# A decoder trunk on one core: four pairs of weight buffers and three fetch buffers instead of three and four, two slots less, and one small fetch moved

## The chip, the cores and the metric

The kernel runs on one NeuronCore of a Trainium2 chip. The core has a matrix engine (TensorE, PE in the profile, with PEld for its weight loads), a vector engine (VectorE, DVE), an engine for activation functions (ScalarE, ACT), a general one (GpSimd, POOL) and a queue engine (SyncE, SP) that only issues DMA transfers. The metric is the device time of one execution in microseconds (us); lower is better. A kernel is timed in several runs, and the median is given.

## The reference

One layer of a hybrid decoder over 512 tokens of width 1024, in float32. `mixed` stands for the three token mixers that share one input projection:

```python
h = rms_norm(x, norm_mix)
z_rnn, z_q, z_k, z_v, z_g, z_dec, z_mq, z_gate = split(h @ w_in)
# 1: recurrence: conv of width 4, gates of 8 blocks, scan over the tokens
xr = causal_dwconv(z_rnn, rnn_conv_w, rnn_conv_b)
out_a = rg_lru(xr, rg_w_a, rg_b_a, rg_w_x, rg_b_x, rg_lambda)
# 2: gated linear attention, 4 heads of 96, values of 192
log_alpha = log_sigmoid(z_dec @ gla_w_decay + gla_b_decay) / 16
o = chunked_gla(z_q, z_k, z_v, log_alpha)
out_b = rms_norm(o, gla_norm) * silu(z_g)
# 3: attention of 4 heads of 192 to a memory of 256 rows
out_c = softmax_attention(z_mq, rms_norm(mem, mem_norm) @ w_mem_kv)
proj = [out_n @ w_branch[n] for n in range(3)]
x = x + sum(sigmoid(z_gate[n]) * proj[n]) @ w_out
# gated MLP of width 3072 with a causal conv of width 3
up = causal_dwconv(rms_norm(x, norm_ffn) @ w_up, ffn_conv_w, ffn_conv_b)
x = x + (gelu(gate_half(up)) * value_half(up)) @ w_down
return rms_norm(x, final_norm)
```

`z_dec` has 16 columns per token, and `gla_w_decay` is a matrix of 16 x 384: the decay logits' weights.

## The kernel before, in words

**Heads and rests.** Each float32 operand is split into a head, rounded to the format that PE multiplies fast (`hi`, `whi`), and the rest (`lo`, `wlo`). A product is made of three matmuls: head by head, head by rest, rest by head (`mm3`, L104). `split` makes the head with a copy on ACT (L97) and the rest with a subtraction on DVE (L98).

**Units and steps.** The program is first laid out as a list `prog` of units and steps. A unit is one block of weights with its matmuls, for instance 128 output channels of a projection: 24 matmuls of 512 columns. `fetch` (L166) takes a fetch buffer (`raw`, 4 KB a partition, `NRAW` = 4 of them), issues the load on SP's queue, takes a pair `whi`, `wlo` (`NWB` = 3 pairs) and splits into it. `emit` places this fetch and split `AHEAD` = 2 units before the unit that uses them, and the steps (evacuations, scans, norms) stand between the units. From this order the framework's scheduler makes the order on each engine at compile time; it may put a later instruction first where an earlier one isn't ready by its own reckoning. On the chip each engine works through its own fixed order. A buffer is taken again when the last reader of what lay in it is done.

**Slots.** All other large intermediates share one pool of `NSLOT` = 53 slots of 2 KB a partition (`fslot` for float32, `rslot` for heads and rests).

**Products with seven multiplications.** The values (`wv`), the gate of the linear attention (`wg`) and most of the down projection are computed by blocks with seven products instead of eight (`seven`, L285 on). Weights are needed singly (`direct`, L303, into a fetch buffer) and as sums of quarters: `load` (L294) fetches a quarter into two slots on SP's queue, and `add` (L299) adds further quarters in flight, as an accumulating DMA on POOL's queue. For `wv` and `wg` the direct quarters are fetched 4 units ahead (`far`). The heads' sums on the other side are made and split on DVE and ACT (L774 to L791, `h_ready`).

**Order of the stages.** Memory keys and values; input projections with the attention to the memory woven between; the recurrence, woven with the gates and projections of the third branch (`b2`); then the stage of the linear attention, in which `wv` and `wg` are woven with gates and projections of the first branch (`g0`, `p0`); then the rest of the branches, the output projection, the up and the down projections.

**The decay weights.** At the start of the linear attention's stage stands the step `decay_weights` (L865 to L873). It takes a slot of 80 rows, clears it on POOL (L867), loads the 16 x 384 matrix three times into it from SP's queue (L869), makes the head on ACT (L871) and the rest of the last 16 rows on DVE (L873). The first matmul with it is `decay_logit` (L894), some 100 us later. The recurrence's stage ends with `lru_decay(1)` (exponentials on ACT), `lru_square`, `lru_root` and `lru_scan` for the blocks 4 to 7; the scan's results are copied on POOL's queue into other rows (L730).

Of the kernel before, what the change touches and what calls it, by code (L numbers as in the profile page):

```python
# [27 lines left out]
H = 4  # L28
DK = 96
DV = 192  # L30
CH = 64
LOW = 16
KZ = 5 * LOW
# [1 line left out]
NF = FF // P  # L35
EPS = 1e-6
LRU_C = 8.0
NSLOT = 53
NWB = 3
AHEAD = 2  # L40
BRANCHES = (2, 0, 1)
NRAW = 4
HT = S // 2
NWARM = 9

# [12 lines left out]
def trunk(ctx: ExitStack, tc: tile.TileContext, x, xT, mem, memT, par, wdecay, wch, wv, wg, wmk,  # L58
          wmv, wrg, wbr, wout, wup, wdown, wdown2, gffn, gfin, out):
    nc = tc.nc  # L60
    pool = lambda name, bufs, **kw: ctx.enter_context(tc.tile_pool(name=name, bufs=bufs, **kw))
    const = pool("const", 1)
    wpool = pool("wpool", NWB)
    hpool = pool("hpool", 1)
    apool = pool("apool", NSLOT)
    small = pool("small", 4)
# [5 lines left out]
    def nm(s):  # L72
        uid[0] += 1
        return f"{s}_{uid[0]}"

    def fslot(shape=(P, S)):
        return apool.tile(list(shape), F32, tag="s", name=nm("f"))

    def rslot(shape=(P, S)):
        return apool.tile(list(shape), F32R, tag="s", name=nm("r"))  # L80
# [14 lines left out]
    def split(hi, lo, src, eng=None):  # L95

        nc.scalar.activation(hi, src, AF.Copy)  # L97
        (eng or nc.vector).tensor_tensor(out=lo, in0=src, in1=hi.bitcast(F32), op=ALU.subtract)  # L98
# [34 lines left out]
    def unit(dram, n, fn, parts=1):  # L133

        w = {}
        i = sum(1 for k, *_ in prog if k == "unit")

        def ready():
            w["w"] = fetch(dram, n, parts)
            for h in behind.get(i, ()):  # L140
                h()
        prog.append(("unit", [(AHEAD, ready)], lambda: fn(w["w"])))
# [5 lines left out]
    def step(fn):  # L148
        prog.append(("step", [], fn))

    def weave(units, steps, lead=0):

        done, m = 0, max(1, len(units) - lead)
        for i, u in enumerate(units):
            unit(*u)
            upto = len(steps) * max(0, i + 1 - lead) // m
            for s in steps[done:upto]:
                step(s)
            done = max(done, upto)
        for s in steps[done:]:  # L160
            step(s)

    def fetch(dram, n, parts):
        p = dram.shape[0]
        raw = wpool.tile([p, n], F32, tag="raw", name=nm("raw"), bufs=NRAW)
        loads.append(nc.sync.dma_start(raw, dram))  # L166
# [118 lines left out]
    def seven(src, n, np, lhs, pre, read, far=AHEAD):  # L285
# [15 lines left out]
        def direct(q, p):  # L301
            raw[q, p] = wpool.tile([P, 2, n], F32, tag="raw", name=nm("raw"), bufs=NRAW)
            loads.append(nc.sync.dma_start(raw[q, p], src(q, p)))  # L303
# [93 lines left out]
    def start():  # L397

        raw = [wpool.tile([P, D], F32, tag="raw", name=nm("raw"), bufs=NRAW) for _ in range(2)]
        whi, wlo = ([wpool.tile([P, D], F32R, tag=t, name=nm(t)) for _ in range(2)] for t in ("whi", "wlo"))  # L400
# [38 lines left out]
    def mem_load(i):  # L439

        raw = wpool.tile([P, 4, MEM], F32, tag="raw", name=nm("raw"), bufs=NRAW)
        nc.sync.dma_start(raw, memT[:, 4 * i:4 * i + 4, :])
# [247 lines left out]
    def lru_decay(g):  # L690
        bs = range(4 * g, 4 * g + 4)
        for b in bs:
            lru["aw", b] = fslot((DK, S)), fslot((DK, S))
            nc.scalar.activation(lru["aw", b][0], lru[0, b], AF.Exp, scale=lsc[:DK, b:b + 1])
        for b in bs:
            r = lru[0, b]
            lru["last"] = nc.scalar.activation(r, r, AF.Tanh, scale=nsc[:DK, b:b + 1])
# [7 lines left out]
    def lru_root(g):  # L705
        with tc.issue_after(lru["last"].ins):
            for i in range(4):
                w = lru["aw", 4 * g + i][1]
                nc.scalar.activation(w, w, AF.Sqrt)
# [22 lines left out]
    def lru_out(t):  # L732
        oa.append((rslot(), rslot()))
        split(*oa[t], of[t])

    each = lambda fn, bs: [lambda b=b: fn(b) for b in bs]
    lo, hi = range(4), range(4, 8)
    b2 = [u for d in range(KD) for u in branch(2, oc, d)]
# [5 lines left out]
    weave([lru_weights(1)] + b2[4:8], each(lru_square, lo) + [lambda: lru_root(0)] + each(lru_split, hi))  # L744
    weave(b2[8:12], [s for p in zip(each(lru_scan, lo), each(lru_gates, hi)) for s in p])
    step(lambda: lru_decay(1))
    weave(b2[12:], each(lru_square, hi) + [lambda: lru_root(1)] + each(lru_scan, hi))


    HP = 2 * DV  # L750
    flat2 = lambda a: a.rearrange("p a b -> p (a b)")
    gla = {}
    vt = [[None, None] for _ in range(NT)]
    sg = [[None, None] for _ in range(NT)]
    chm = const.tile([DK, S], F32, name="chm")
# [105 lines left out]
    def g_fast():  # L861
        return seven(lambda q, p: wg[p, int(q[1]) - 1, int(q[2]) - 1], HP, 2, h_lhs, {}, g_read, 4)


    def decay_weights():  # L865
        wy = fslot((KZ, H, DK))
        nc.gpsimd.memset(wy, 0.0)  # L867
        for c in range(0, KZ, 2 * LOW):
            nc.sync.dma_start(wy[c:c + LOW], wdecay)  # L869
        r = gla["wy"] = rslot((KZ, H, DK))  # L870
        nc.scalar.activation(r, wy, AF.Copy)  # L871
        lo = slice(4 * LOW, KZ)
        nc.vector.tensor_tensor(out=r[lo], in0=wy[lo], in1=r[lo].bitcast(F32), op=ALU.subtract)  # L873
# [144 lines left out]

    step(causal)
    step(decay_weights)  # L1020
    gates = {}

# [340 lines left out]
```

## Time and profile before

| | |
|---|---|
| median of 3 runs | 940.94 us (940.58 to 941.29) |
| the profiled execution | 941.12 us, of it span 939.4 us |
| granted clock of PE, mean | 0.996 |
| PE busy | 921.3 us, 98% |
| DVE, ACT, POOL busy | 636.6, 488.2, 90.9 us |
| DMA | 116.93 MB, 124 GB/s over the span |

The span runs from the first to the last instruction. A row of a timeline has the start and the duration in us, the engine, the line, the operation, what it writes and reads, and in brackets the idle time of the engine before it with what ended it. PE is busy in 98% of the span, so the time is to be looked for in the few stretches where it isn't, and in the granted clock there.

### The profile page before, as it was taken

Reading aid. Unit: us, or ns where it says so; the run is one execution under the profiler, and the core shown is the slowest. Engines: PE = TensorE matmul, PEld = TensorE weight load, DVE = VectorE, ACT = ScalarE, POOL = GpSimd, SP = SyncE. Lnnn points to the kernel's source line nnn. Section 1 sums busy time; section 2 is a strip of 40 time slices with the busy share of each in tenths; the row PEclk is TensorE's granted clock in tenths of the full one; section 3 lists DMA queues with packets and bytes.
Section 4 is the critical chain, followed back from the end, with each engine's and each line's share of the span. In section 5 each row is a group of like instructions: output and inputs, shape, how many; then the busy total and the mean of one; then the engine's idle time right before and its main releaser. Section 6 shows DMA issues by size and latency. Waiting matters only on the chain.

```text
span 939.4 us, 11996 instructions
## 1 busy us (share of the span) xinstructions
PE 921.3 (98%) x4390; PEld 779.7 (83%) x4390; DVE 636.6 (68%) x1117; ACT 488.2 (52%) x796; POOL 90.9 (10%) x133
## 2 busy tenths in 40 slices
PE   9999999999998999999999999999999999999996
PEld 7899888888877998878888898888888888888885
DVE  6996745565788454795767665555686666698765
ACT  6765555685845345864434424344345444545544
POOL 0000000000053141000000000000010130012102
PEclk9999999999999999999999999999999999999999
DMA  7435223213369594231146401233364685357612
GB/s 250 160 119 196 88 80 108 85 59 106 111 161 186 130 202 135 76 119 51 51 135 225 167 23 45 92 111 112 135 114 138 146 227 119 110 126 184 162 45 89
DMA packets 45562, 116.93 MB, mean 124 GB/s; under 512 B 5520, under 2 KB 12864, under 8 KB 45504
## 3 DMA queue, kind: packets, MB, share of 16 engines
q1 hardware_dynamic: 33152, 94.28, 30.3%
q0 software_dynamic: 11776, 20.85, 13.0%
q10 hardware_dynamic: 576, 1.05, 0.3%
q8 instruction: 34, 0.56, 0.2%
q14 instruction: 24, 0.20, 0.1%
HBM read 111.69 MB, written 3.67 MB: 123 GB/s over the span
## 4 chain that ended last, share of the span: by engine, by line
PE 88%; DVE 6%; ACT 3%; issue 1%; DMA 1%; POOL 0%; SPq 0%; DVEq 0%; ACTq 0%
PE mm L104 81%; PE sm L104 2%; PE mm L419 1%; DVE wlo L98 1%; PE sm L983 1%; DMA m<-in_xT 1%; DVE f L920 0%; PE sm L969 0%; PE sm L604 0%; PE sm L985 0%; PE sm L585 0%; DVE f L774 0%; DMA f<-in_wdecay 0%; DVE r L98 0%; PE sm L956 0%
## 5 line engine op out<-in xcount | busy, mean ns | idle before, releaser
L98 DVE TENSOR_TENSOR wlo<-raw,whi 128x1024 fp32r<-128x1024 f32 (+2 forms) x155 | 172.4, 1115 | 161.0 <-PE mm L104 75.7
L97 ACT ACTIVATE whi<-raw 128x1024 fp32r<-128x1024 f32 (+2 forms) x155 | 149.7, 970 | 173.2 <-PE mm L104 159.5
L104 PE MATMUL mm<-whi,r 128*128 128x512 f32 (+2 forms) x568 | 172.7, 374 | 3.5 <-ACT r L97 1.8
L104 PE MATMUL mm<-h2l,whi 128*128 128x512 f32 x360 | 140.1, 389 | 0.0
L104 PE MATMUL mm<-h2h,whi 128*128 128x512 f32 x360 | 139.9, 389 | 0.0
L104 PEld LDWEIGHTS mm<-whi,r 128*128 128x128 f32 x568 | 106.4, 189 | 19.3 <-DVE r L98 2.3
L104 PE MATMUL mm<-hh,whi 128*128 128x512 f32 x288 | 113.8, 395 | 2.3 <-ACT whi L97 2.3
L104 PE MATMUL mm<-hl,whi 128*128 128x512 f32 x288 | 113.0, 392 | 0.0
L104 PE MATMUL mm<-wlo,r 128*128 128x512 f32 (+2 forms) x284 | 106.2, 374 | 0.4 <-DVE wlo L98 0.4
L104 PE MATMUL mm<-r,whi 128*128 128x512 f32 (+1 forms) x448 | 98.9, 369 | 0.0
L104 PEld LDWEIGHTS mm<-r,whi 128*128 128x128 f32 x448 | 77.8, 189 | 14.1 <-DVE r L98 0.2
L104 PE MATMUL mm<-h2h,wlo 128*128 128x512 f32 x360 | 88.9, 389 | 0.0
L97 ACT ACTIVATE whi<-f 128x512 fp32r<-128x512 f32 (+2 forms) x90 | 48.3, 581 | 74.6 <-PE mm L104 64.5
L104 PEld LDWEIGHTS mm<-h2h,wlo 128*128 128x128 f32 x360 | 67.6, 188 | 14.0
L104 PEld LDWEIGHTS mm<-h2l,whi 128*128 128x128 f32 x360 | 67.6, 188 | 14.0
L104 PEld LDWEIGHTS mm<-h2h,whi 128*128 128x128 f32 x360 | 67.5, 188 | 14.0
L98 DVE TENSOR_TENSOR wlo<-f,whi 128x512 fp32r<-128x512 f32 (+2 forms) x90 | 53.7, 631 | 35.8 <-ACT whi L97 19.6
L299 POOL DMA_DIRECT2D f<-in_wdown x40 | 35.1, 986 | 438.9 <-DVE wlo L98 415.8
L1127 DVE SCALAR_TENSOR_TENSOR f<-mm,prm,f 128x511 f32<-128x511 f32 x96 | 71.4, 745 | 6.9 <-ACT f L1125 6.1
L104 PE MATMUL mm<-hh,wlo 128*128 128x512 f32 x288 | 71.2, 389 | 0.0
L104 PEld LDWEIGHTS mm<-hh,whi 128*128 128x128 f32 x288 | 54.1, 188 | 13.9 <-ACT whi L97 3.0
L104 PEld LDWEIGHTS mm<-hh,wlo 128*128 128x128 f32 x288 | 54.1, 188 | 11.3
(243 smaller groups left out, 1313.2 us busy)
## 6 DMA issues: line engine op xcount, KB each, us to landing
raw<-in_wup SPq DMA_DIRECT2D x48, 512.0 KB, 3.6
raw<-in_wch SPq DMA_DIRECT2D x40, 512.0 KB, 3.6
f<-in_wdown POOLq DMA_DIRECT2D x40, 256.0 KB, 5.3
raw<-in_wbr SPq DMA_DIRECT2D x24, 384.0 KB, 3.1
raw<-in_wdown SPq DMA_DIRECT2D x14, 512.0 KB, 3.7
f<-in_wdown SPq DMA_DIRECT2D x20, 256.0 KB, 4.3
raw<-in_wout SPq DMA_DIRECT2D x8, 512.0 KB, 3.4
f<-in_wv POOLq DMA_DIRECT2D x16, 200.0 KB, 5.6
```

Source lines behind the costliest of these rows:

```text
L97: nc.scalar.activation(hi, src, AF.Copy)
L98: (eng or nc.vector).tensor_tensor(out=lo, in0=src, in1=hi.bitcast(F32), op=ALU.subtract)
L104: nc.tensor.matmul(ps, lhsT=l, rhs=r, start=first and i == 0, stop=last and i == len(seq) - 1, skip_group_check=more)
L299: nc.gpsimd.dma_start(raw[to, p][j], src(q, p)[:, j, :], accum_op=ALU.add)
L419: nc.tensor.matmul(ps[u], lhsT=a, rhs=b, start=q == 0 and i in (0, 2), stop=q == KD - 2 and i >= len(seq) - 2)
L983: nc.tensor.matmul(ps[:, j, :], lhsT=sT[h][:, t, :], rhs=vt[t][hp][:, j, :], start=True, stop=t == 0)
L1127: nc.vector.scalar_tensor_tensor(out=a[:, j:], in0=ps[:, :S - j], scalar=col(C_FCW + 48 * (2 - j) + f), in1=a[:, j:], op0=ALU.mult, op1=AL ...
```

## The change

Four edits. `NWB` goes from 3 to 4: a fourth pair of buffers for heads and rests of weights, 8 KB more a partition. `NRAW` goes from 4 to 3 (4 KB less) and `NSLOT` from 53 to 51 (4 KB less), so that the memory used is the same. The clearing and the three loads of the decay weights go into a new step `decay_load`, which stands in the recurrence's stage after `lru_decay(1)`; the loads are issued on POOL's queue instead of SP's. `decay_weights` keeps its place and its two instructions on ACT and DVE.

```diff
-NSLOT = 53
-NWB = 3
+NSLOT = 51
+NWB = 4
 AHEAD = 2
 BRANCHES = (2, 0, 1)
-NRAW = 4
+NRAW = 3
...
+    gla = {}
+
+
+    def decay_load():
+        wy = gla["raw"] = fslot((KZ, H, DK))
+        nc.gpsimd.memset(wy, 0.0)
+        for c in range(0, KZ, 2 * LOW):
+            nc.gpsimd.dma_start(wy[c:c + LOW], wdecay)
+
...
     step(lambda: lru_decay(1))
+    step(decay_load)
     weave(b2[12:], each(lru_square, hi) + [lambda: lru_root(1)] + each(lru_scan, hi))
...
     def decay_weights():
-        wy = fslot((KZ, H, DK))
-        nc.gpsimd.memset(wy, 0.0)
-        for c in range(0, KZ, 2 * LOW):
-            nc.sync.dma_start(wy[c:c + LOW], wdecay)
+        wy = gla.pop("raw")
         r = gla["wy"] = rslot((KZ, H, DK))
         nc.scalar.activation(r, wy, AF.Copy)
```

More of the change, by code (lines that the diff above doesn't have):

```diff
@@ L751, in trunk @@
     flat2 = lambda a: a.rearrange("p a b -> p (a b)")
-    gla = {}
     vt = [[None, None] for _ in range(NT)]
```

## The prediction

> **What bounds the kernel now.** I read the totals first, then the busy time of the engines by stretches of 20 us, then each engine's timeline where the first engine shows idle time.
>
> ```profile
> span 939.4 us, 11996 instructions
> PE 921.3 (98%) x4390; PEld 779.7 (83%) x4390; DVE 636.6 (68%) x1117; ACT 488.2 (52%) x796; POOL 90.9 (10%) x133
> ...
> 260.00:280.00 20.00, 18.61 (x91) 16.34 (x89) 17.21 (x27) 8.30 (x15) 9.05 (x17) 1.00 0.70 179
> 280.00:300.00 20.00, 16.40 (x73) 14.21 (x74) 17.04 (x35) 12.36 (x23) 9.83 (x12) 0.91 0.95 178
> 300.00:320.00 20.00, 18.85 (x99) 17.56 (x98) 12.75 (x29) 7.30 (x14) 3.52 (x4) 1.00 0.36 85
> 400.00:420.00 20.00, 18.36 (x93) 14.97 (x92) 19.57 (x32) 12.76 (x19) 1.99 (x4) 1.00 0.32 110
> 600.00:620.00 20.00, 20.00 (x90) 16.57 (x89) 10.23 (x13) 8.53 (x10) 0.00 (x0) 1.00 0.29 99
> ```
>
> The columns are PE, PEld, DVE, ACT and POOL busy, granted clock, DMA share and GB/s. TensorE (PE) is idle for 18.1 us of the whole span. Most of the rest of the span looks like the last row, full to 20.00, where neither buffers nor fetches can give anything. What can be won lies in the four rows before it: 1.39, 3.60, 1.15 and 1.64 us of idle PE, and a clock of 0.91 in the second. The idle stretches of more than half a microsecond, on PE's timeline (start, duration, then idle time before and its releaser):
>
> ```profile
> 269.07 0.50 PE L104 MATMUL mm<-hh,whi 128*128 128x512 f32 x1 [1.15 <-ACT whi L97]
> ...
> 281.32 0.81 PE L104 MATMUL mm<-whi,r 128*128 128x400 f32 x3 [0.75 <-DVE r L98]
> 285.04 0.45 PE L104 MATMUL mm<-whi,r 128*128 128x400 f32 x1 [1.78 <-ACT r L97]
> 286.99 1.37 PE L104 MATMUL mm<-whi,r 128*128 128x400 f32 x3 [0.95 <-DVE r L98]
> 304.26 0.50 PE L104 MATMUL mm<-hh,whi 128*128 128x512 f32 x1 [1.15 <-ACT whi L97]
> 415.47 0.47 PE L946 MATMUL sm<-ident,f 96*128 96x96 f32 x3 [1.64 <-DVE f L934]
> ```
>
> The two waits of 1.15 are for a head of weights just split; the three between 281 and 287 are for splits late on ACT and DVE. Why those are late stands on the two engines:
>
> ```profile
> 247.91 1.78 ACT L97 ACTIVATE whi<-raw 128x768 fp32r<-128x768 f32 x2
> 265.78 0.87 ACT L97 ACTIVATE whi<-raw 128x800 fp32r<-128x800 f32 x1 [3.06 <-PE mm L104]
> 267.96 1.06 ACT L97 ACTIVATE whi<-raw 128x1024 fp32r<-128x1024 f32 x1 [1.31 <-PE mm L104]
> 271.25 0.53 ACT L871 ACTIVATE r<-f 80x384 fp32r<-80x384 f32 x1 [2.23 <-DMA f<-in_wdecay]
> 303.15 1.06 ACT L97 ACTIVATE whi<-raw 128x1024 fp32r<-128x1024 f32 x1 [1.21 <-PE mm L104]
> ...
> 248.78 0.96 DVE L98 TENSOR_TENSOR wlo<-raw,whi 128x768 fp32r<-128x768 f32 x1 [2.58 <-ACT whi L97]
> 266.69 1.35 DVE L98 TENSOR_TENSOR wlo<-raw,whi 128x800 fp32r<-128x800 f32 x1 [1.30 <-ACT whi L97]
> 269.05 1.23 DVE L98 TENSOR_TENSOR wlo<-raw,whi 128x1024 fp32r<-128x1024 f32 x1 [0.55 <-ACT whi L97]
> 271.81 0.55 DVE L873 TENSOR_TENSOR r<-f,r 16x384 fp32r<-16x384 f32 x1 [0.93 <-ACT r L871]
> ```
>
> An ACT split that waits for PE has its raw weights and waits for a matmul to free one of the three pairs. The split at 267.96 starts 0.04 us after PE's last matmul before the gap of 1.15, so PE waits for a buffer that it has itself just freed. DVE, between 249 and 287, is nearly without a gap except those it inherits: 1.30 and 0.55 from late heads, 0.93 from the decay logits' weights.
>
> **The change part by part.** The sum is made against the profiled execution: 941.12 us, 939.4 of it span. The median of the runs is 940.94, 0.18 lower, well inside the 0.2% (1.9 us) that a measurement here can tell from no change.
>
> *Fourth pair, 260 to 287.* A split may start one unit earlier. On DVE the gaps of 1.30 and 0.55 go. One rest, the 0.96 at 248.78, can also move into the 2.58 idle before it, out of the crowded part, since its head need no longer queue behind the gates' exponentials on ACT. That is 1.30 + 0.55 + 0.96 = 2.81.
>
> *Decay weights, same stage.* Removed from SP: three DMA issues.
>
> ```profile
> 266.62 1.25 SPq L869 DMA_DIRECT2D f<-in_wdecay  x3
> 256.18 1.53 POOL L730 DMA_DIRECT2D f<-f  x3 [88.27 <-DVE wlo L98]
> ```
>
> In the new place POOL clears the tile and issues three DMAs, about 0.45 + 1.53 us by its own rows of that size (an estimate), inside its 88 us of idle time. If that cover is gone, those 2 us stand ahead of the scan's copies (L730), which gate nothing before the heads' splits 40 us later; ends 0 and 2.0, I take 0. Behind the old wait stood ACT's whole queue for 2.23 and DVE's for 0.93. ACT has slack (8.30 busy of 20), so I count DVE's 0.93. The split L871/L873 itself stays.
>
> PE resumes at 286.99 on a DVE result, so DVE's gain, 2.81 + 0.93 = 3.74, is PE's there. Ends: 0.93, if the fourth pair is not used, and 4.99, the 1.39 and 3.60 of the first two rows, all of it before that point.
>
> *The clock.* After those waits the granted clock falls:
>
> ```profile
> 286.00:288.00 2.00, 1.05 (x4) 1.01 (x4) 2.00 (x4) 0.51 (x1) 0.34 (x1) 0.61 1.07 167
> 288.00:290.00 2.00, 2.00 (x8) 1.98 (x7) 0.62 (x2) 0.00 (x0) 0.00 (x0) 0.54 1.01 254
> ```
>
> The loss is 0.39 x 1.05 + 0.46 x 2.00 = 1.3 us. With 4.99 - 3.74 = 1.25 of idle time left, spread over 20 us, I expect no drop: the 1.64 idle before 415.47 left its row at 1.00. Gain 1.3, ends 0 and 1.3. The Trainium skill (TensorE: Matmul & The Clock Gate, HAM oscillation) puts the drop down to idle gaps over about 3.4 us; no single gap here is over 1.78, so by that rule these waits aren't the cause and the 1.3 would stay lost. The trace has 0.75 + 1.78 + 0.95 = 3.48 us of idle PE within 6.4 us right ahead of the drop, and goes against the rule as worded.
>
> *Fourth pair at 304.26.* The head's split at 303.15 waited 1.21 for PE; one unit earlier it is hidden. Gain 1.15, ends 0 and 1.15.
>
> *Fourth pair at 415.* DVE is the chain there:
>
> ```profile
> 384.73 1.29 DVE L918 TENSOR_TENSOR f<-f,f 96x512 f32<-96x512 f32 x2 [3.32 <-ACT f L907]
> 394.01 0.94 DVE L98 TENSOR_TENSOR wlo<-raw,whi 128x768 fp32r<-128x768 f32 x1
> ```
>
> One more rest fits into the 3.32 idle, so 0.94 leaves the chain before PE's wait of 1.64. Gain 0.9, ends 0 and 1.64. Three fetch buffers pull the other way: the raw load that now starts four splits ahead starts three ahead. In a full stretch 90 matmuls take 20.00 us, so a unit of 24 takes 5.3, and a landing fits into it; I take 0.
>
> ```profile
> raw<-in_wch SPq DMA_DIRECT2D x40, 512.0 KB, 3.6
> ```
>
> *Two slots less.* Slots run out in one place that I can see, where SP waits for splits of the heads' sums to free them:
>
> ```profile
> SPq L294 <- DVE r L98: 5.2, 3, 4.9
> ...
> 297.31 2.13 SPq L294 DMA_DIRECT2D f<-in_wg  x4
> ```
>
> Two of these four loads will wait for later releases; each release is the end of a split on DVE, and the wait already seen is up to 4.9. They start the gate product's sums, which reach PE at about 345 with nothing to spare:
>
> ```profile
> 344.60 0.53 ACT L97 ACTIVATE whi<-f 128x384 fp32r<-128x384 f32 x1 [1.72 <-DMA f<-in_wg]
> 320.00:346.00 26.00, 26.00 (x140) 24.52 (x139) 13.22 (x21) 10.84 (x19) 9.72 (x11) 1.00 1.00 235
> ```
>
> DMA is full (share 1.00) and ACT waits for the sums, but PE isn't idle yet: if PE comes earlier, part of the gain is given back. Ends 0 and 4.9; I take 1.5, nearer to 0 because the releasing splits come earlier as well.
>
> Sum: 3.74 + 1.3 + 1.15 + 0.9 - 1.5 = 5.6; 941.12 - 5.6 = 935.5.
>
> **The rivals.**
>
> *The gate product's sums hold PE.* All that is won up to 305 (3.74 + 1.3 + 1.15) is waited away at 345, since the DMA share is 1.00 there; only the 0.9 and perhaps 1 us remain: 939.5. For it: the two rows above. Against it: between 300 and 320 the DMA share is 0.36, so the chain can start sooner when its heads are split sooner.
>
> *The pair isn't used.* ACT and DVE run in order, and the scheduler may leave the splits where they were, behind the same evacuations that wait for the same matmuls. Then only the decay wait goes: 941.12 - 0.93 = 940.2. Against it: the waits on ACT show a free engine waiting for nothing but a pair.
>
> *The clock drops all the same.* The idle time that is left may suffice for it, or it has another cause: 935.5 + 1.3 = 936.8.
>
> *Three fetch buffers block SP: slower.* Directly fetched quarters sit in raw buffers from four units ahead, and SP is in order.
>
> ```profile
> 270.30 0.35 SPq L166 DMA_DIRECT2D raw<-in_wch  x1
> 270.70 1.85 SPq L294 DMA_DIRECT2D f<-in_wv  x4
> 283.24 0.99 DVE L98 TENSOR_TENSOR wlo<-raw,whi 128x800 fp32r<-128x800 f32 x1
> 279.27 7.07 POOL L299 DMA_DIRECT2D f<-in_wv  x8 [9.90 <-DVE wlo L98]
> f<-in_wv POOLq DMA_DIRECT2D x16, 200.0 KB, 5.6
> 298.52 0.97 ACT L97 ACTIVATE whi<-f 128x400 fp32r<-128x400 f32 x2 [0.54 <-PE mm L104]
> 304.59 0.34 PE L104 MATMUL mm<-whi,r 128*128 128x400 f32 x1
> ```
>
> The fetch at 270.30 has its buffer from a split just before; with one buffer less it waits for the split that ends at 284.23, 13.9 us later, and the four loads of the value product behind it too. Their sums now land at 286.34 + 5.6 = 291.9 for a split at 298.52, a slack of 6.6. So they come 13.9 - 6.6 = 7.3 us too late at the split. PE uses it at 304.59, 6.1 us after its start; head and rest need about 1.9 of that (an estimate from the 0.97 of the head), which leaves 4.2, a stall of 3.1, and none of the gains up to 305: 941.12 + 3.1 - 0.9 = 943.3. It decides from the point where SP gets past that fetch later than 270.3 + 6.6 + 4.2 = 281. Against it: the splits themselves come earlier, and the loads may be ordered ahead of the fetch.
>
> The Trainium skill speaks against one hope in the move to POOL's queue (DMA: Bandwidth & Descriptors, Issuing engines are not separate DMA queues): the issuing engine saves only issue time. It agrees with my counting nothing but a wait.
>
> **How the numbers follow.** Likeliest, 0.48: 935.5, with its own range 931.5 (all 7.8 us of idle time in the four rows and the clock's 1.3, rounded) to 938.5 (half the gain). Sums hold PE, 0.15, 939.5, split evenly by the line at 939.06. Clock drops all the same, 0.12, 936.8. Pair not used, 0.12, 940.2. SP blocked, 0.13, 943.3. Faster by over 0.2%: 0.48 + 0.12 + 0.07 = 0.67; within: 0.08 + 0.12 = 0.20; slower: 0.13. The range 931.5 to 941.5 leaves out the blocked case and a little below.
>
> **What would show it.** Right: the waits at 269, 304 and on the decay weights gone, the clock at 1.00 from 280 to 300, L871 without a DMA wait, PE past the value product's third group about 4 us sooner. Wrong: PE idle near 340 to 346 behind DMA of in_wg (first rival); ACT's splits still 0.04 us behind a matmul with the same idle times (second); SP's in_wv loads after 281 (the slower one). New idle time in the stretches that are now full, from instructions ordered anew, would break the sum in a way that I can't price.

## The result, and the profile after

| | before | after |
|---|---|---|
| median | 940.76 us (939.25 to 941.29, 4 runs) | 933.80 us (933.06 to 934.49, 4 runs) |
| the profiled execution | 941.12 us, span 939.4 | 933.06 us, span 931.4 |
| granted clock of PE, mean | 0.996 | 0.998 |

The ratio after to before is 0.9941, with a 95% interval of 0.9925 to 0.9957: some 5.5 us faster, three times what a measurement here can tell from no change. The medians of the table lie 7.0 us apart because these four runs of before came out high: in the experiments below before has medians of 939.2 to 939.4, and the changed kernel, timed again, 933.71. Totals and stretches of the changed kernel, in the order of columns of the prediction's first fence:

```profile
span 931.4 us, 12010 instructions
PE 917.0 (98%) x4390; PEld 776.8 (83%) x4390; DVE 636.0 (68%) x1117; ACT 486.8 (52%) x796; POOL 92.2 (10%) x136
...
260.00:280.00 20.00, 19.29 (x98) 17.53 (x98) 19.97 (x36) 11.58 (x21) 11.92 (x19) 1.00 0.79 179
280.00:300.00 20.00, 18.87 (x95) 16.78 (x94) 18.48 (x32) 10.88 (x22) 4.41 (x6) 1.00 0.86 194
300.00:320.00 20.00, 20.00 (x104) 18.43 (x103) 10.10 (x23) 8.60 (x16) 5.48 (x7) 1.00 0.64 147
320.00:346.00 26.00, 26.00 (x138) 24.28 (x137) 14.85 (x26) 10.45 (x19) 9.12 (x11) 1.00 0.83 188
400.00:420.00 20.00, 18.53 (x108) 15.65 (x107) 17.21 (x27) 14.73 (x22) 0.00 (x0) 1.00 0.34 107
```

Between 260 and 280 DVE goes from 17.21 to 19.97 busy, so the 2.8 us of gaps that DVE inherited are filled. Between 280 and 300 PE's clock is 1.00 instead of 0.91, and from 300 to 320 PE is full. PE's timeline shows which waits are left (start, duration, then idle time before and its releaser):

```profile
45.31 0.61 PE L228 MATMUL sm<-ones,f 128*128 128x1 f32 x4 [0.50 <-DVE f L460]
58.89 2.17 PE L104 MATMUL mm<-r,whi 128*128 128x256 f32 x16 [0.33 <-DVE f L481]
...
279.33 1.21 PE L104 MATMUL mm<-r,whi 128*128 128x512 f32 x4 [0.71 <-ACT whi L97]
282.83 0.99 PE L104 MATMUL mm<-whi,r 128*128 128x400 f32 x4 [0.82 <-DVE r L98]
284.59 0.42 PE L104 MATMUL mm<-whi,r 128*128 128x400 f32 x1 [0.30 <-DVE f L830]
...
402.74 0.91 PE L951 MATMUL sm<-ident,f 96*128 96x96 f32 x9
406.30 0.47 PE L951 MATMUL sm<-ident,f 96*128 96x96 f32 x3 [1.47 <-DVE f L939]
```

The two waits of 1.15 are gone, and those inside the value product's stretch shrink: 6.14 us of idle time between 260 and 305 become 1.83 (waits of over a quarter of a microsecond). Two small waits at 45 and 59 are new. The wait of 1.64 before the transposes is now 1.47.

To see where the time was won, I counted PE's matmuls in the traces (4390 in each) and took the time in us at which the next one behind the first N ends:

```
N                       100     400    1300    1500    1900    4300
before                28.99   75.87  267.02  315.63  397.15  911.42
after                 26.57   74.33  265.46  307.84  389.07  903.15
decay fetch alone     27.11   73.95  265.10  313.84  395.93  910.13
3 fetch buffers alone 27.12   73.99  265.13  311.84  393.37  907.54
51 slots alone        26.94   73.79  264.87  312.86  394.38  908.62
four fetch buffers    27.82   74.50  265.63  307.99  389.21  903.28
```

The first lead isn't the change's: before's profiled execution lost about 1.9 us in its first 100 matmuls, which other kernels with three pairs don't. Of that lead, 1.54 is left behind the 400th. From the 1300th to the 1500th it grows by 6.23, to 7.79, and by 0.5 after that.

### The profile page after: what moved, and what is told of

Read it like the earlier page. It is cut to its first block, busy times and chain, and to the rows that moved or that the text cites. A ratio compares the mean times of both kernels' runs of the same rounds, so it can differ in the third digit from the quotient of the medians.

```text
span 931.4 us, 12010 instructions
## 1 busy us (share of the span) xinstructions
PE 917.0 (98%) x4390; PEld 776.8 (83%) x4390; DVE 636.0 (68%) x1117; ACT 486.8 (52%) x796; POOL 92.2 (10%) x136
## 3 DMA queue, kind: packets, MB, share of 16 engines
q10 hardware_dynamic: 576, 1.05, 0.3%
## 4 chain that ended last, share of the span: by engine, by line
PE 88%; DVE 6%; ACT 2%; DMA 2%; issue 1%; SPq 0%; DVEq 0%; ACTq 0%
PE mm L104 83%; PE sm L104 2%; DVE wlo L98 1%; DMA m<-in_xT 1%; DVE r L98 1%; PE sm L988 1%; DMA raw<-in_memT 1%; DVE f L925 0%; DMA raw<-in_wmk 0%; PE sm L974 0%; PE sm L990 0%; PE sm L585 0%; DVE f L221 0%; ACT whi L97 0%; PE sm L961 0%
```

## The experiments

Each ratio is to the kernel before, timed beside it (medians there 939.2 to 939.4 us). The diffs of the parts are against before, the later ones against the changed kernel.

**The parts, one at a time.** The pairs with what pays for their memory, without the moved fetch:

```diff
-NSLOT = 53
-NWB = 3
-NRAW = 4
+NSLOT = 51
+NWB = 4
+NRAW = 3
```

> Four pairs, three fetch buffers, 51 slots; the decay weights fetched where they were. Theory (the pairs carry the gain, the moved fetch is worth one DVE wait of 0.93): PE's two waits of 1.15 at 269 and 304 are gone, one wait on the decay weights stays, clock at 1.00 after it; about 934.7 us. Rival (the moved fetch carries most of it): most of the idle time between 280 and 287 stays, 938 to 940.

Measured: 934.72 us (934.36 to 935.51), ratio 0.9954 [0.9942, 0.9966]. Most of the gain is here. What is missing stands on PE and ACT:

```profile
273.33 0.45 PE L104 MATMUL mm<-whi,hh 128*128 128x400 f32 x1 [1.40 <-ACT f L812]
...
268.75 0.53 ACT L871 ACTIVATE r<-f 80x384 fp32r<-80x384 f32 x1 [1.22 <-DMA f<-in_wdecay]
272.35 0.54 ACT L97 ACTIVATE whi<-f 128x400 fp32r<-128x400 f32 x1 [1.65 <-DMA f<-in_wv]
272.79 0.88 ACT L812 ACTIVATE f<-mm 128x400 f32<-128x400 f32 x2
```

PE waits for an evacuation (L812) that stands in ACT's order behind two splits waiting for DMAs. The prediction had counted a wait of DVE's here; on top of four pairs it is ACT's queue that holds PE up.

The moved fetch alone (three pairs, four fetch buffers, 53 slots):

```diff
+    step(decay_load)
...
-            nc.sync.dma_start(wy[c:c + LOW], wdecay)
+            nc.gpsimd.dma_start(wy[c:c + LOW], wdecay)
```

> Only the decay weights' fetch moved; three pairs, four fetch buffers, 53 slots. Theory: PE still waits 1.15 for a head at about 269 and 304, DVE gains 0.93, the clock still drops: 939.5 to 940. Rival (the moved fetch carries most): PE resumes 4 us sooner at the place of 287 and the clock stays up: 935 to 936.

Measured: 939.57 us, 0.9998 [0.9987, 1.0009]. The DMA wait on ACT is gone, and DVE waits all the same:

```profile
263.86 0.87 ACT L97 ACTIVATE whi<-raw 128x800 fp32r<-128x800 f32 x1 [3.07 <-PE mm L104]
264.64 0.51 ACT L876 ACTIVATE r<-f 80x384 fp32r<-80x384 f32 x1
...
265.18 1.08 DVE L878 TENSOR_TENSOR r<-f,r 16x384 fp32r<-16x384 f32 x1 [1.12 <-ACT r L876]
```

The decay weights' head on ACT now stands behind a split that waits 3.07 us for a pair. The two effects don't add: without the fourth pair the move gives nothing, with it about 1.0 us. The medians differ by that (934.72 against 933.71 below, with overlapping intervals), and so do PE's waits of over a quarter of a microsecond between 260 and 305: 2.84 us in the pairs-only kernel, 1.83 in the changed one. The move to POOL's queue and the earlier place weren't tried apart.

The two payments, each alone:

```diff
-NRAW = 4
+NRAW = 3
```

> Only the fetch buffers go from four to three; pairs and slots as before. Theory (a landing fits into a unit, the lost buffer costs nothing): within 0.5 us of before, 940.3 to 941.3. Rival 1 (fetches come late, SP blocked): new idle PE at 280 to 305, 942 to 944. Rival 2 (the 1.55 us that the changed kernel gained in its first 30 us come from fewer fetches that compete there): 939.3, with the hundredth matmul ending at about 26.6 instead of 29.0 us.

Measured: 938.71 us, 0.9999 [0.9989, 1.0009].

```diff
-NSLOT = 53
+NSLOT = 51
```

> Only the slots go from 53 to 51. The prediction charged 1.5 us for this (ends 0 and 4.9), by loads of the gate product that wait longer for slots: 942.4 by that charge. Theory now (the loads are early enough): no difference, 940.3 to 941.3, the wait of SP for slots longer but PE not idle at 340 to 346.

Measured: 939.12 us, 0.9997 [0.9986, 1.0007]. Neither costs anything with three pairs.

**The changed kernel again, and its neighbours.** The changed kernel beside three variants of it:

> The changed kernel itself, once more on the chip of the other three. Theory (of the 8.0 us between the two profiled spans, 1.55 are the start of the one profiled execution of before and no effect of the change): a ratio of 0.993 to 0.995, 5 to 6 us; its hundredth matmul ends at 26.5 to 27.2 us as in the four part kernels. Rival (the change itself shortens the start): ratio 0.991 to 0.992.

Measured: 933.71 us (933.11 to 934.85), 0.9943 [0.9928, 0.9959].

Four pairs and four fetch buffers, 51 slots:

```diff
-NRAW = 3
+NRAW = 4
```

> The changed kernel with four fetch buffers in place of three, slots kept at 51. Theory (the lost fetch buffer costs nothing): within 0.5 us of the changed kernel, 933.3 to 934.5. Rival (three fetch buffers cost something that the pairs hide): 931 to 932.5, with less idle PE between 279 and 285.

Measured: 932.83 us (932.40 to 933.18), 0.9931 [0.9917, 0.9945]. The intervals overlap; the trace says where the difference is. From the 100th to the 400th matmul this kernel takes 46.7 us and the changed one 47.8, and its stretch from 40 to 60 is full, without the waits at 45 and 59:

```profile
40.00:60.00 20.00, 20.00 (x157) 19.39 (x157) 19.68 (x46) 13.46 (x23) 1.89 (x9) 1.00 0.45 139
```

Four pairs, four fetch buffers, six slots less:

```diff
-NSLOT = 51
-NRAW = 3
+NSLOT = 47
+NRAW = 4
```

> Four pairs, four fetch buffers, the decay fetch moved, and 47 slots, four less than in raw4_slots51 (932.8). The prediction charged 1.5 us for the first two slots. Theory (the loads that wait for slots are early enough): within 0.5 us of 932.8. Rival (slots are what made the kernel with five pairs and 47 slots slow): 936 or more, with PE idle at about 274.

Measured: 932.98 us (932.79 to 933.37), 0.9927 [0.9916, 0.9939]: as with 51. With four pairs the slots have room; the next kernel pays with slots too.

Five pairs:

```diff
-NSLOT = 51
-NWB = 4
+NSLOT = 47
+NWB = 5
```

> Five pairs, three fetch buffers, 47 slots, the decay weights' fetch moved. Theory (what is left between 279 and 285 is work of DVE and no wait for a pair): no gain over the changed kernel, 933.5 to 935, the idle PE there still for rests and heads of the sums (DVE and ACT, not a pair). Rival (pairs are still short): 931.5 to 932.5. A second rival, the slots: 47 are too few and SP waits for them, 935.5 or more.

Measured: 940.22 us (937.08 to 942.56), 1.0011 [0.9999, 1.0022]. The whole gain is gone. Only the rival that blames the slots had allowed for such a time, and the trace shows another cause. PE's and ACT's timelines, and PE's stretch:

```profile
273.96 0.70 PE L104 MATMUL mm<-whi,hh 128*128 128x400 f32 x1 [4.30 <-ACT f L821]
...
271.11 0.54 ACT L97 ACTIVATE whi<-f 128x400 fp32r<-128x400 f32 x1 [4.46 <-DMA f<-in_wv]
272.98 0.54 ACT L97 ACTIVATE whi<-f 128x400 fp32r<-128x400 f32 x1 [1.33 <-DMA f<-in_wv]
273.42 0.88 ACT L821 ACTIVATE f<-mm 128x400 f32<-128x400 f32 x2
...
270.00:280.00 10.00, 6.04 (x22) 6.00 (x23) 7.02 (x12) 3.25 (x6) 5.17 (x6) 0.66 0.76 158
```

With a fifth pair free, the scheduler put two more splits of summed quarters ahead of the evacuation L821, which in the changed kernel stands at 267.33, ahead of such splits at 272.01. Their DMAs haven't landed, ACT is in order, and PE stands 4.30 us for the evacuation; the clock falls to 0.66 of full speed in that stretch. It is the wait of the pairs-only kernel again, three times as long. Neither slots nor fetch buffers made the DMAs late: the value product's last loads go out at 264.53 and 273.73, in the changed kernel at 264.21 and 273.91. This wait isn't all: of the 6.5 us between the two kernels' medians some 1.5 are lost earlier, where PE waits 1.05 us at 106.94 for ACT (L591), which the changed kernel doesn't do.

**The second cause: DVE's load between 247 and 290.** The first sums of the heads' sides for the value product (`h_sum1`: three adds and subtractions on DVE for each of two halves) are pulled out of that stretch, into the recurrence's stage:

```diff
     step(decay_load)
+    for p in range(2):
+        step(lambda p=p: h_sum1(p))
...
-        pre["c1"].append((7, h_sum1))
```

> The changed kernel with the first six sums of the heads' quarters (about 4.1 us of DVE) made in the recurrence's stage, where DVE waits for ACT's exponentials. Theory (DVE's work between 247 and 290 is what is left of the bound): PE's 1.8 us of idle time at 279 to 285 shrink to under 0.5, 932.0 to 932.8. Rival (ACT or the DMA sums hold PE there): the same idle time with another releaser, 933.5 to 934.2.

Measured: 931.97 us (931.23 to 934.17), 0.9925 [0.9909, 0.9942]. PE's waits between 260 and 305 shrink from 1.83 to 0.69 + 0.64. The same edit without the pairs (three pairs, four fetch buffers, 53 slots):

> Three pairs, four fetch buffers, 53 slots, with the decay fetch moved and the six sums early. Theory (two causes: a pair that PE itself frees, 1.15 at about 267 and again at 302; and DVE's load, the 3.2 us between 278 and 286): the two waits of 1.15 stay, the others shrink to under 1, 935.5 to 937. Rival 1 (the pairs alone make all of it): 938.5 to 940. Rival 2 (DVE's load alone makes all of it, and the waits of 1.15 go with it): 932.5 to 934.

Measured: 934.73 us (933.95 to 935.93), 0.9949 [0.9937, 0.9961], just better than the theory's range and short of the second rival's. PE's timeline:

```profile
266.75 0.50 PE L104 MATMUL mm<-hh,whi 128*128 128x512 f32 x1 [1.15 <-ACT whi L97]
282.17 0.73 PE L104 MATMUL mm<-r,whi 128*128 128x512 f32 x2 [0.71 <-ACT whi L97]
290.15 0.51 PE L104 MATMUL mm<-r,whi 128*128 128x512 f32 x1 [0.44 <-ACT r L97]
297.32 0.50 PE L104 MATMUL mm<-hh,whi 128*128 128x512 f32 x1 [1.15 <-ACT whi L97]
```

This tells the two causes apart. The waits of 1.15 need a pair, and no DVE work taken away helps them. Those of 280 to 287 (3.84 before) shrink with less DVE work ahead of them (0.71 + 0.44 are left); the fourth pair gave DVE its own idle time back, which comes to nearly the same.

All three together, `h_sum1` early with four pairs and four fetch buffers:

> Four pairs, four fetch buffers, 51 slots, the decay weights' fetch moved, and the first six sums early: the two things that helped, together. Theory (with four pairs the third fetch buffer's loss cost about 0.9 us by two waits at 45 and 59, and the sums another 1.7 at 279 to 285, independent of each other): both groups of waits gone, 930.8 to 931.6. Rival (they meet in the same wait): 931.8 to 932.5.

Measured: 931.24 us (930.69 to 932.33), 0.9910 [0.9897, 0.9923], the fastest version here, 2.5 us below the changed kernel. PE by stretches, and its one wait over half a microsecond from 225 on to 425:

```profile
260.00:280.00 20.00, 20.00 (x103) 18.20 (x102) 18.82 (x33) 12.49 (x22) 11.89 (x16) 1.00 0.88 194
280.00:300.00 20.00, 20.00 (x102) 18.17 (x101) 17.89 (x33) 11.57 (x23) 3.48 (x4) 1.00 0.81 196
...
403.83 0.47 PE L952 MATMUL sm<-ident,f 96*128 96x96 f32 x3 [1.49 <-DVE f L940]
```

For that last wait, the five rests of the weights woven into the stretch ahead of it were given to POOL in the kernel just above:

```diff
-    weave(p0[3:], [qk_back] + each(decay_apply, heads))
+    weave([u + (3,) for u in p0[3:]], [qk_back] + each(decay_apply, heads))
```

> The kernel early_raw4 with the rests of the five projections of the decay stage made on POOL in place of DVE. Theory (DVE's chain from the logarithms to the transposes is the wait of 1.5 us at about 406): DVE loses about four rests of 0.95 there, the wait goes, 929.5 to 930.2. Rival (POOL is slow at it, or slows DVE while both read the same memory): 931 to 933.

Measured: 937.36 us (936.15 to 939.87), 0.9978 [0.9969, 0.9988]: slower than without the edit by 6 us. DVE's and POOL's timelines, then PE's and PE's stretch:

```profile
380.69 2.93 DVE L924 TENSOR_TENSOR f<-f,f 96x512 f32<-96x512 f32 x2
383.54 3.98 DVE L926 TENSOR_TENSOR_SCAN f<-chm,f 96x512 f32<-96x512 f32 x2
...
380.29 2.17 POOL L98 TENSOR_TENSOR wlo<-raw,whi 128x768 fp32r<-128x768 f32 x1 [4.47 <-ACT whi L97]
382.97 2.36 POOL L98 TENSOR_TENSOR wlo<-raw,whi 128x768 fp32r<-128x768 f32 x1 [0.50 <-ACT whi L97]
...
402.07 0.30 PE L952 MATMUL sm<-ident,f 96*128 96x96 f32 x1 [0.75 <-DVE f L940]
407.48 1.70 PE L952 MATMUL sm<-ident,f 96*128 96x96 f32 x9 [5.12 <-DVE f L940]
...
400.00:420.00 20.00, 14.14 (x81) 12.16 (x80) 16.71 (x27) 13.36 (x20) 1.94 (x4) 0.83 0.44 145
```

A rest takes POOL 2013 ns and DVE 0.96 us. The rival's second half is what the trace shows: beside POOL's rests at 380.29 and 382.97 the same DVE instructions that take 1.28 and 2.33 us in the kernel without this edit take 2.93 and 3.98. These 3.3 us are more than the 1.7 that DVE saves by two rests less in its chain up to the transposes. Beyond the 0.66 us by which all of PE is later here, the chain starts 1.4 us later, behind one more table load on ACT, and its last result for the transposes comes 3.0 us later (407.43 in place of 403.77). PE's new order adds to it: nine transposes stand right behind the one at 402.07, with no matmul between, though what they read comes from DVE 5.4 us after what that one read; in the kernel without this edit five matmuls stand in such a place. PE's idle time there grows from 1.49 to 0.75 + 5.12, and the clock of the stretch falls to 0.83. The two causes weren't tried apart.

## Why the prediction was right, and where its steps were not

The forecast was 935.5 us against 941.12; the median came out at 933.80, inside the range, by the likeliest case. Most of the 1.7 us between the two is the base: before's profiled execution was some 1.8 us above its later medians. The gain itself came out as forecast, 5.5 against 5.6, but three of its terms were off, and that they cancel is luck. (The low end of the likeliest case doesn't come out either: 941.12 less 7.8 and 1.3 is 932.0, not 931.5.) The sum, term by term:

*Fourth pair and decay weights up to 287, the clock, the wait at 304: 3.74 + 1.3 + 1.15 = 6.19.* Right as a sum: the lead grows by 6.23 from the 1300th to the 1500th matmul. The idle time falls by 4.31 (4.89 was expected). Some 0.6 of that is this one execution of before: three fetch buffers alone and 51 slots alone, with the same three pairs and the fetch unmoved, have 5.46 and 5.50 us of idle time there, not 6.14. Of the other 1.92 about 1.3 is the clock: two kernels with the same waits, one with the drop, differ by that (last section). Some 0.6 I could not place. Step by step, on the two engines:

```profile
248.97 1.22 DVE L98 TENSOR_TENSOR wlo<-raw,whi 128x1024 fp32r<-128x1024 f32 x1
261.92 1.89 DVE L98 TENSOR_TENSOR wlo<-raw,whi 128x800 fp32r<-128x800 f32 x2
264.42 1.38 DVE L878 TENSOR_TENSOR r<-f,r 16x384 fp32r<-16x384 f32 x1
...
260.29 0.87 ACT L97 ACTIVATE whi<-raw 128x800 fp32r<-128x800 f32 x1 [4.16 <-PE mm L104]
261.06 0.51 ACT L876 ACTIVATE r<-f 80x384 fp32r<-80x384 f32 x1
```

DVE's rests no longer wait for heads. The rest of 0.96 left the crowded part as reckoned and stands at 236.81, though DVE still idles 2.52 us ahead of 247.16. The decay weights' split waits neither for its DMA (L876) nor for ACT (L878). ACT still waits for PE, now ahead of need. The 0.93 for the decay weights was put on the wrong engine and taken to add; alone it was worth 0, with four pairs about 1.0.

*The clock, 1.3.* Right here: two-microsecond stretches that read 0.61 and 0.54 now read 1.00 with the 1.83 of idle time that is left.

```profile
286.00:288.00 2.00, 2.00 (x13) 2.00 (x12) 0.81 (x2) 0.90 (x2) 1.44 (x2) 1.00 1.10 301
288.00:290.00 2.00, 2.00 (x13) 2.00 (x12) 1.91 (x5) 0.79 (x3) 1.46 (x2) 1.00 1.10 196
```

But it isn't the fixed cost it was booked as; see the last section.

*The wait at 415, 0.9.* Too large. The chain on DVE from its first weighting of a head to the transposes shrank as reckoned, from 30.7 us (384.73 to 415.47) to 29.9 (376.42 to 406.30), with one rest less in it. But PE's wait only went from 1.64 to 1.47. Before, PE's nine transposes ahead of the wait were these:

```profile
410.81 0.91 PE L946 MATMUL sm<-ident,f 96*128 96x96 f32 x9
```

From their end to the wait PE had 2.11 us of matmuls (411.72 to 413.83); after the change 1.18 (403.65 to 404.83). The rest of them now come behind the wait, and what DVE saved went to the order on PE. The lead grows by 0.5 from the 1500th to the 4300th matmul, more than the wait alone gives.

*Two slots less, +1.5.* The step that failed. Slots cost nothing: not two of them with three pairs, nor four more with four pairs (51 to 47). SP does wait longer for them, 9.7 us in place of 5.2, as the table of waits of SP's queue shows (total, times, longest):

```profile
SPq L294 <- DVE r L98: 9.7, 2, 9.5
...
292.21 1.98 SPq L294 DMA_DIRECT2D f<-in_wg  x4
```

Yet the loads go out at 292.21, before it was 297.31, and PE is full from 320 to 346. The argument took a wait of SP's for a delay of PE's without asking how early SP had come to it. The rival that the sums hold PE at 345 falls by the same row.

*Three fetch buffers, 0.* Right with three pairs, wrong with four: 0.9 us between the medians (933.71 against 932.83), lost between the 100th and the 400th matmul, where I hadn't looked, since before shows hardly any idle PE there (0.11 us from 40 to 60). The misses, 1.5 too much lost for the slots, 0.9 too little for the fetch buffer and 0.4 too much won at 415, nearly cancel, which is why the gain fits.

*SP blocked.* Its first half came true:

```profile
264.21 0.90 SPq L294 DMA_DIRECT2D f<-in_wv  x2
273.49 0.33 SPq L166 DMA_DIRECT2D raw<-in_wbr  x1
273.91 0.91 SPq L294 DMA_DIRECT2D f<-in_wv  x2
279.26 0.33 SPq L166 DMA_DIRECT2D raw<-in_wch  x1
```

The fetches of `wbr` and `wch` are issued 5.4 and 9.0 us later than before. But all loads of the value product were ordered ahead of the late one, two of them far ahead, and the last go out at 273.91, before the deciding 281. The counter-argument had named this.

*New waits from instructions ordered anew* were called what couldn't be priced. In the changed kernel they are the 0.83 at 45 and 59; one pair further they are the whole gain.

## What to carry to other kernels

A buffer more pays where the profile shows an engine waiting for a buffer just in front of a wait of the bound engine, and at no more than those waits are worth; here a second way to the same idle time, work taken off the engine in between, was worth nearly as much (4.8 us against 5.9, each on top of the moved fetch), and both together more. After each buffer added, read the in-order queues again: splits that may start earlier can be put ahead of an evacuation before their DMA has landed, and one pair too many gave back everything. Before handing an engine's work to another, ask what the other will slow: rests moved to POOL cost DVE more than they saved. A queue that waits longer is a cost only from the point where someone waits for what stands behind it.

## What the runs showed of the hardware that was not expected

The clock fell in one profiled execution and not in another with nearly the same idle time. PE by stretches, three fetch buffers alone, then 51 slots alone:

```profile
276.00:286.00 10.00, 6.79 (x35) 5.50 (x33) 9.85 (x23) 6.43 (x13) 7.05 (x8) 1.00 0.86 143
286.00:296.00 10.00, 10.00 (x49) 8.75 (x50) 8.26 (x14) 7.16 (x14) 3.48 (x4) 1.00 1.02 226
...
276.00:286.00 10.00, 6.79 (x31) 5.78 (x30) 9.54 (x21) 6.21 (x11) 7.05 (x8) 0.91 0.88 146
286.00:296.00 10.00, 10.00 (x48) 8.90 (x47) 8.03 (x14) 6.19 (x12) 3.48 (x4) 0.92 0.89 186
```

Both have 6.79 us of busy PE and a longest single wait of 1.78; one keeps 1.00, the other drops to 0.91 and 0.92, and is 1.3 us longer from the 1300th to the 1500th matmul (47.99 against 46.71). With the fetch alone the idle time is the same, 5.47, its longest wait 1.35, and the clock stood at 0.71, 0.50, 0.50 and 0.58 in the four stretches of 2 us from 282 on: 48.74 for the same matmuls, 2.0 more than without a drop. The times of before spread over 937.1 to 942.1 us, those of the changed kernel over 933.1 to 934.9. The Trainium skill (TensorE: Matmul & The Clock Gate, What's actually happening) has the gate watch a free-running window of about 3.4 us; a window that falls differently on the same waits would give this. That fits and wasn't shown, and a longest wait of 1.78 with a drop goes against the single gaps of over 3.4 us that its section on oscillation asks for.

DVE's subtraction of 16x384 took 1.38 us at 264.42, 0.55 before. GpSimd works beside it on another tile:

```profile
264.37 1.02 POOL L773 TENSOR_SCALAR_AFFINE_SELECT f<-f 128x512 f32<-128x512 f32 x1
```

The select ends at 265.39, and 0.55 more is 265.94; DVE's instruction ends at 265.80. The Trainium skill (SBUF — State Buffer, SBUF: two separate sides) says that a DVE instruction with two inputs in SBUF is blocked by a GpSimd instruction that reads SBUF and started first, until that one is done; the row agrees within 0.14 us. No wait of PE's was seen behind it. With the rests on POOL the same stands on the way to PE's longest wait: POOL's rest ends at 382.46, 1.28 more is 383.74, and DVE's two subtractions end at 383.62; the next rest ends at 385.33, 2.33 more is 387.66, and the two scans end at 387.52.
